# Where the exponents of a scan's weights lie, and which engine multiplies them by the weights

## The chip, the cores and the metric

The kernel runs on one core of a Trainium2 chip. A time is the device time of one execution in microseconds (us). The kernel before has a median of 2456.4 us over 3 runs (2455.82 to 2459.3).

## The reference, cut to what matters

One encoder layer runs on two requests with shared weights: a long one (prompt, 1024 tokens) and a short one (sample, 512 tokens). Half of its heads are a state space mixer with a scan in both directions, half are dilated attention; an output projection, a cross attention on 256 memory tokens and an MLP follow. All is in float32. The change lies in the scan, which goes over chunks of 128 tokens, one direction at a time, here forwards:

```python
a_cs = jnp.cumsum(dt * A.reshape(g, r), axis=2)
xdt = x * dt[..., None]
causal = jnp.tril(jnp.ones((q, q), dtype=bool))[:, :, None, None]
seg = a_cs[:, :, :, None] - a_cs[:, :, None, :]
lmat = jnp.where(causal, jnp.exp(jnp.where(causal, seg, 0.0)), 0.0)
cb = jnp.einsum('bcign,bcjgn->bcijg', Cm, Bm)
y_diag = jnp.einsum('bcijg,bcijgr,bcjgrp->bcigrp', cb, lmat, xdt)
...
y_off = jnp.einsum('bcign,bcgrpn,bcigr->bcigrp', Cm, prev, jnp.exp(a_cs))
return (y_diag + y_off).reshape(bsz, l, h, p)
```

There are 2 groups of 4 heads. The weights of a head inside a chunk, `cb * lmat * dt` summed over both directions, are a 128x128 matrix.

## The kernel before, in words

Dense work (projections, cross attention, MLP) runs on TensorE (PE) in three matmuls for each product, a high and a low part of every operand. Their weights arrive by DMA in pieces of 128x512 (`raw`), ScalarE (ACT) rounds them to the high part `whi` (L190), and VectorE (DVE) and GpSimd (POOL) take turns at the low part `wlo` (L192). The mixers are generators that are woven into this dense work: after so many dense steps comes one step of the mixer. The mixers run one after the other: scan of the short request, its attention, scan of the long one, its attention. The program text gives priorities only. A planner with its own timeline model (`schedule_with_timeline_sim=True`) orders the instructions of each engine before the program is built, and puts in the waits; on the chip each engine then works through its list in that order.

PSUM has eight banks of 128x512: three for dense sums (`mm`), two for transposes (`tp`), and one each for the tags `a`, `b`, `c` that the mixers share (`mx_bank`, tiles `ma`, `mb`, `mc`). A new tile of a tag waits until the last one of it has had its last reader.

In the scan, `ssd`, the short request has 4 chunks and the long one 8. The backward states come first. Then for every chunk c, in four steps:

1. `inside(c, 0)`: the first group's weights times the chunk's tokens, four heads, into bank `c` (`py`, L647). The rows of the next chunk's first group are asked for (`rows_of`, a DMA of 512 KB that spreads one row over 128 partitions, L628; its tile `se` has two buffers).
2. `inside(c, 1)` into the same bank; `masks` of the next chunk (bank `b`, L619 and L622); the rows of its second group; DVE adds the bank to `y` (L690); the carried state's part goes through bank `a` (`outside`, L656, L658).
3. `weigh(c + 1, 0)`: the weights of the next chunk's first group; the backward state's part through bank `b`.
4. `update` of the carried state (L594, L600, L601), `weigh(c + 1, 1)`, then the gate and the norm of the chunk (L702 to L708).

`weigh` has a tile `e` of 128x2x4x128: `e[:, 0]` holds the forward row sums, `e[:, 1]`, also called `w`, the backward ones, for each of four heads. For each head ACT makes the forward exponent in place (L635, Identity with a bias), DVE takes the smaller of it and the backward exponent (L636), ACT (L637) and DVE (L638) fill `w` with the masked products. Then one exponential over the four heads on ACT (L639) and one product `w * exp` on POOL (L640).

Of the kernel before, what the change touches and what calls it, by code (L numbers as in the profile page):

```python
# [13 lines left out]
AF = mybir.ActivationFunctionType  # L14
OP = mybir.AluOpType
# [69 lines left out]
def encoder(ctx: ExitStack, tc: tile.TileContext, I, y_p, y_s):  # L85
    nc = tc.nc
# [19 lines left out]
    def mx_bank(tag):  # L106
        return ps_mx.tile([128, 512], F32, name="m" + tag)
# [430 lines left out]
    def ssd(st, pool):  # L538
# [34 lines left out]
        def load(c, full):  # L573
            sl = slice(c * 128, c * 128 + 128)
            x = pool.tile([128, 512], F32, name="sx", bufs=2)
            nc.sync.dma_start(x, st.xs[sl, :])
            bt = pool.tile([128, 256], F32, name="sbt", bufs=2)
            nc.sync.dma_start(bt, st.bt[sl, :])
            if not full:
                return x, bt  # L580
            bc = pool.tile([128, 4, 128], F32, name="sbc", bufs=2)
            nc.sync.dma_start(bc, st.bc[:, sl].rearrange("(k p) t -> p k t", p=128))
            return x, bt, bc
# [21 lines left out]
        for c in range(nt - 1, 0, -1):  # L605
            x, bt = load(c, False)
# [23 lines left out]

        def weigh(c, g, cbm, e):
            w = e[:, 1]
            for h in range(4):
                col = [v[:, c, d * 8 + g * 4 + h:d * 8 + g * 4 + h + 1] for v in (nacs, st.dt) for d in range(2)]
                nc.scalar.activation(e[:, 0, h], e[:, 0, h], AF.Identity, bias=col[0])  # L635
                nc.vector.scalar_tensor_tensor(e[:, 0, h], w[:, h], col[1], e[:, 0, h], op0=OP.add, op1=OP.min)  # L636
                nc.scalar.activation(w[:, h], cbm[:, 1, g], AF.Identity, scale=col[3])  # L637
                nc.vector.scalar_tensor_tensor(w[:, h], cbm[:, 0, g], col[2], w[:, h], op0=OP.mult, op1=OP.add)  # L638
            nc.scalar.activation(e[:, 0], e[:, 0], AF.Exp)  # L639
            nc.gpsimd.tensor_tensor(w, w, e[:, 0], op=OP.mult)  # L640
            weights[c, g] = w

        def inside(c, g, py):
# [22 lines left out]
        for g in range(2):  # L666
            weigh(0, g, cbm, rows_of(0, g))
            yield
        for c in range(nt):
            nxt = c + 1 < nt  # L670
            sl = slice(c * 128, c * 128 + 128)
            x, bt, bc = tiles[c]
# [20 lines left out]
            if nxt:  # L693
                weigh(c + 1, 0, cbm, e0)
# [4 lines left out]
            if nxt:  # L699
                carry = update(carry, xs, bt, c, 0)  # L700
                weigh(c + 1, 1, cbm, e1)
# [584 lines left out]
```

## Time and profile before

| | |
|---|---|
| median of 3 runs | 2456.4 us |
| the profiled execution | 2455.78 us |
| its span, first to last instruction | 2454.0 us |
| PE busy | 2393.4 us (98%) |
| DVE busy | 1410.0 us (57%) |
| ACT busy | 967.3 us (39%) |
| POOL busy | 736.3 us (30%) |
| granted TensorE clock, mean | 0.993 |

A share over the whole span says little here, as the stages differ: the scans run in about 110 to 245 us (short request) and 545 to 735 us (long request), attention and dense work in the rest. A line of the profile names the line of the kernel (L640), the engine, and the tile written and read (`se<-se`). "Idle before" is the time in which the engine did nothing just before these instructions, with what ended it. DMAs are issued by the queue of SyncE (SP).

### The profile page before, as it was taken

The numbers are of one execution on the slowest core, as the hardware profiler recorded it, in microseconds if no ns is written. First come the engines' busy times: TensorE is split into PE (matmuls) and PEld (weight loads), VectorE is DVE, ScalarE is ACT, GpSimd is POOL, SyncE is SP. The second block draws the span as 40 slices with busy tenths as digits, with TensorE's granted clock in tenths as the row PEclk, the third lists the DMA queues.
The fourth block names the chain that finished last, engine by engine and source line by source line (L and its number), as shares of the span: only waits on it lengthen the run. The fifth ranks groups of instructions, "written<-read, shape, count | busy, mean of one in ns | idle before, by whom it ended". The sixth has DMA issues, their size and how long they took to land.

```text
span 2454.0 us, 34361 instructions
## 1 busy us (share of the span) xinstructions
PE 2393.4 (98%) x12323; PEld 2005.8 (82%) x12323; DVE 1410.0 (57%) x2834; ACT 967.3 (39%) x2337; POOL 736.3 (30%) x604
## 2 busy tenths in 40 slices
PE   7999999998889999999999999999999999999999
PEld 6877788887668997888878889999888888888887
DVE  7787677647885567556555635555534344344444
ACT  5465455445555556344423325334411212212111
POOL 3353214425542132333344212111222322222221
PEclk9999999999989999999999999999999999999999
DMA  5665345557766453344253411111111111211111
GB/s 184 192 213 191 118 136 148 147 170 245 239 234 177 111 142 93 105 122 112 74 191 104 172 35 53 56 56 44 35 52 35 52 52 39 65 35 52 52 35 69
DMA packets 253082, 272.00 MB, mean 111 GB/s; under 512 B 43090, under 2 KB 200048, under 8 KB 252912
## 3 DMA queue, kind: packets, MB, share of 16 engines
q1 hardware_dynamic: 252912, 269.82, 35.5%
q8 instruction: 97, 1.59, 0.3%
q14 instruction: 73, 0.60, 0.1%
HBM read 215.55 MB, written 54.20 MB: 110 GB/s over the span
## 4 chain that ended last, share of the span: by engine, by line
PE 78%; DMA 6%; DVE 5%; ACT 1%; issue 1%; SPq 1%; POOL 0%; ACTq 0%; DVEq 0%; POOLq 0%
PE mm L205 16%; PE mm L206 16%; PE mm L207 16%; PE tp L205 7%; PE tp L207 7%; PE tp L206 7%; PE mc L812 3%; PE ma L783 2%; DMA se<-acp 1%; PE mb L799 1%; DVE wlo L192 1%; PE tp L224 1%; DVE se L636 1%; DMA se<-acs 1%; DVE se L638 1%
## 5 line engine op out<-in xcount | busy, mean ns | idle before, releaser
L192 POOL TENSOR_TENSOR wlo<-raw,whi 128x512 fp32r<-128x512 f32 x240 | 361.5, 1521 | 520.7 <-ACT whi L190 447.9
L1138 DVE TENSOR_TENSOR h<-mm,h 128x512 f32<-128x512 f32 x384 | 262.6, 687 | 405.8 <-PE mm L207 405.3
L205 PE MATMUL mm<-whi,chi 128*128 128x512 f32 (+1 forms) x1088 | 397.1, 366 | 8.8 <-ACT chi L230 5.6
L206 PE MATMUL mm<-wlo,chi 128*128 128x512 f32 (+1 forms) x1088 | 392.2, 361 | 0.0
L207 PE MATMUL mm<-whi,clo 128*128 128x512 f32 (+1 forms) x1088 | 392.1, 363 | 0.0
L190 ACT CAST whi<-raw 128x512 fp32r<-128x512 f32 x480 | 268.2, 618 | 249.9 <-PE tp L206 115.8
L192 DVE TENSOR_TENSOR wlo<-raw,whi 128x512 fp32r<-128x512 f32 x240 | 294.3, 1238 | 102.6 <-ACT whi L190 102.2
L205 PE MATMUL mm<-whi,hidh 128*128 128x512 f32 x768 | 305.0, 397 | 0.8 <-DVE h L1138 0.8
L207 PE MATMUL mm<-whi,hidl 128*128 128x512 f32 x768 | 302.9, 394 | 0.0
L206 PE MATMUL mm<-wlo,hidh 128*128 128x512 f32 x768 | 302.5, 394 | 0.0
L205 PE MATMUL tp<-chi,whi 128*128 128x512 f32 x720 | 284.4, 395 | 0.0
L207 PE MATMUL tp<-chi,wlo 128*128 128x512 f32 x720 | 284.3, 395 | 0.0
L206 PE MATMUL tp<-clo,whi 128*128 128x512 f32 x720 | 284.0, 394 | 0.0
L1122 POOL TENSOR_TENSOR hidl<-hr,hidh 128x512 fp32r<-128x512 f32 x96 | 126.0, 1312 | 479.1 <-ACT hidh L1121 298.5
L205 PEld LDWEIGHTS mm<-whi,chi 128*128 128x128 f32 x1088 | 207.1, 190 | 39.2 <-ACT chi L230 7.0
L207 PEld LDWEIGHTS mm<-whi,clo 128*128 128x128 f32 x1088 | 206.5, 190 | 28.6
L206 PEld LDWEIGHTS mm<-wlo,chi 128*128 128x128 f32 x1088 | 206.9, 190 | 27.5
L1121 ACT CAST hidh<-hr 128x512 fp32r<-128x512 f32 x96 | 59.6, 621 | 400.1 <-PE mm L206 325.9
L205 PEld LDWEIGHTS mm<-whi,hidh 128*128 128x128 f32 x768 | 144.5, 188 | 34.1 <-DVE h L1138 1.8
L207 PEld LDWEIGHTS mm<-whi,hidl 128*128 128x128 f32 x768 | 144.4, 188 | 33.6
L206 PEld LDWEIGHTS mm<-wlo,hidh 128*128 128x128 f32 x768 | 144.6, 188 | 32.3
L207 PEld LDWEIGHTS tp<-chi,wlo 128*128 128x128 f32 x720 | 135.4, 188 | 31.5
(285 smaller groups left out, 4109.0 us busy)
## 6 DMA issues: line engine op xcount, KB each, us to landing
raw<-in_mlp_w_dram SPq DMA_DIRECT2D x256, 256.0 KB
raw<-in_w_in_dram SPq DMA_DIRECT2D x96, 256.0 KB
qkp<-ev SPq DMA_DIRECT2D x32, 256.0 KB
raw<-in_xatt_wkv_dram SPq DMA_DIRECT2D x32, 256.0 KB
se<-acp SPq DMA_DIRECT2D x16, 512.0 KB
raw<-in_w_out_dram SPq DMA_DIRECT2D x32, 256.0 KB
ak<-qkp SPq DMA_DIRECT2D x32, 256.0 KB
raw<-in_xatt_wq_dram SPq DMA_DIRECT2D x32, 256.0 KB
```

Source lines behind the costliest of these rows:

```text
L190: nc.scalar.copy(hi[:, sl, sc], raw)
L192: eng.tensor_tensor(lo[:, sl, sc], raw, f(hi[:, sl, sc]), op=OP.subtract)
L205: nc.tensor.matmul(ps, lh, rh, start=start, stop=False)
L206: nc.tensor.matmul(ps, lh, rl, start=False, stop=False)
L207: nc.tensor.matmul(ps, ll, rh, start=False, stop=stop)
L224: nc.tensor.transpose(pt[:, k, t, :], xn[t][:, (2 * kp + k) * 128:(2 * kp + k + 1) * 128], units(2 * kp + k))
L636: nc.vector.scalar_tensor_tensor(e[:, 0, h], w[:, h], col[1], e[:, 0, h], op0=OP.add, op1=OP.min)
L783: nc.tensor.matmul(pq[:, i, :W], qu, ops[i][0][j], start=j == 0, stop=j == 1)
L812: nc.tensor.matmul(po[:, i * 64:i * 64 + 64], pT[:, i * nk + j, :], ops[i][1][j][:, rs], start=j == 0, stop=j == nk - 1)
L1121: nc.scalar.copy(hh[:, ft], r)
L1122: nc.gpsimd.tensor_tensor(hl[:, ft], r, f(hh[:, ft]), op=OP.subtract)
L1138: nc.vector.tensor_tensor(h[t][:, cs], ps, h[t][:, cs], op=OP.add)
```

## The change

The exponents are written to a PSUM tile `x` of tag `c`, the tag of the chunk's sum `py`, instead of back into `e[:, 0]`. ACT writes them there, DVE takes the minimum there, ACT's exponential runs there in place. The product with the weights moves from POOL to DVE, with one input in SBUF and one in PSUM. Everything behind these lines has numbers that are two higher.

```diff
         def weigh(c, g, cbm, e):
             w = e[:, 1]
+
+            x = mx_bank("c").rearrange("p (h i) -> p h i", h=4)
             for h in range(4):
                 col = [v[:, c, d * 8 + g * 4 + h:d * 8 + g * 4 + h + 1] for v in (nacs, st.dt) for d in range(2)]
-                nc.scalar.activation(e[:, 0, h], e[:, 0, h], AF.Identity, bias=col[0])
-                nc.vector.scalar_tensor_tensor(e[:, 0, h], w[:, h], col[1], e[:, 0, h], op0=OP.add, op1=OP.min)
+                nc.scalar.activation(x[:, h], e[:, 0, h], AF.Identity, bias=col[0])
+                nc.vector.scalar_tensor_tensor(x[:, h], w[:, h], col[1], x[:, h], op0=OP.add, op1=OP.min)
                 nc.scalar.activation(w[:, h], cbm[:, 1, g], AF.Identity, scale=col[3])
                 nc.vector.scalar_tensor_tensor(w[:, h], cbm[:, 0, g], col[2], w[:, h], op0=OP.mult, op1=OP.add)
-            nc.scalar.activation(e[:, 0], e[:, 0], AF.Exp)
-            nc.gpsimd.tensor_tensor(w, w, e[:, 0], op=OP.mult)
+            nc.scalar.activation(x, x, AF.Exp)
+            nc.vector.tensor_tensor(w, w, x, op=OP.mult)
             weights[c, g] = w
```

## Rows read from the trace of the kernel before

**Rows 1.** The page, busy time and share of the span by engine.
```profile
PE 2393.4 (98%) x12323; PEld 2005.8 (82%) x12323; DVE 1410.0 (57%) x2834; ACT 967.3 (39%) x2337; POOL 736.3 (30%) x604
```

**Rows 2.** Windows: busy us by engine, granted clock, DMA share, of both scans.
```profile
core 0: us, PE busy (x) PEld busy (x) DVE busy (x) ACT busy (x) POOL busy (x), PEclk, DMA share, GB/s
110.00:245.00 135.00, 127.53 (x622) 104.33 (x621) 105.66 (x224) 80.01 (x185) 67.19 (x67) 0.99 0.63 200
...
545.00:735.00 190.00, 165.74 (x776) 132.37 (x775) 157.27 (x307) 103.92 (x293) 100.49 (x83) 0.94 0.73 241
```

**Rows 3.** Waits of PE in 545:735: us in total, times, longest us.
```profile
PE ma L656 <- DVE carry L601: 5.2, 3, 3.8
PE mc L647 <- POOL se L640: 4.7, 4, 2.3
```

**Rows 4.** Timeline of PE: start, us, instructions, idle time before and what ended it.
```profile
662.19 1.10 PE L647 MATMUL mc<-sx,se 128*128 128x64 f32 x8 [2.29 <-POOL se L640]
...
680.03 1.12 PE L647 MATMUL mc<-sx,se 128*128 128x64 f32 x8 [1.60 <-POOL se L640]
```

**Rows 5.** Windows of 5 us behind these two waits, columns as in rows 2.
```profile
660.00:665.00 5.00, 2.81 (x14) 2.48 (x15) 4.58 (x8) 3.43 (x8) 4.36 (x3) 0.89 0.37 110
665.00:670.00 5.00, 5.00 (x19) 3.97 (x19) 3.14 (x8) 0.95 (x2) 2.32 (x3) 0.77 0.88 215
...
680.00:685.00 5.00, 4.97 (x21) 4.33 (x22) 5.00 (x7) 3.12 (x9) 2.53 (x2) 0.66 0.16 40
```

**Rows 6.** Lines of POOL, 110:245 and 545:735: busy us, mean ns, idle before.
```profile
L640 POOL TENSOR_TENSOR se<-se 128x512 f32<-128x512 f32 x8 | 11.6, 1444 | 11.4 <-DVE se L638 5.0 <-DVE rst L212 4.0 <-ACT ev L522 2.3
...
L640 POOL TENSOR_TENSOR se<-se 128x512 f32<-128x512 f32 x16 | 21.0, 1315 | 25.1 <-DVE se L638 7.3 <-ACT chi L230 6.4 <-ACT ev L906 3.0
```

**Rows 7.** Lines of DVE in 545:735, columns as in rows 6.
```profile
L636 DVE SCALAR_TENSOR_TENSOR se<-se,sa 128x128 f32<-128x128 f32 x64 | 29.1, 504 | 14.3 <-ACT se L635 14.1
L638 DVE SCALAR_TENSOR_TENSOR se<-scbm,dtp,se 128x128 f32<-128x128 f32 x64 | 27.9, 478 | 0.0
L192 DVE TENSOR_TENSOR wlo<-raw,whi 128x512 fp32r<-128x512 f32 x18 | 21.0, 1179 | 3.7 <-ACT whi L190 3.7
...
L690 DVE TENSOR_TENSOR sy<-mc,sy 128x512 f32<-128x512 f32 x8 | 5.4, 681 | 0.6 <-PE mc L647 0.6
```

**Rows 8.** Three lines of DVE, whole span: ns minimum/median/maximum, first and last start.
```profile
L636 DVE SCALAR_TENSOR_TENSOR se<-se,sa x96: 335/343/1430, 117.4 to 723.0; 128x128 f32<-128x128 f32 x96
L638 DVE SCALAR_TENSOR_TENSOR se<-scbm,dtp,se x64: 333/340/1387, 562.2 to 729.2; 128x128 f32<-128x128 f32 x64
...
L587 DVE TENSOR_TENSOR sxs<-sx,sdd x20: 673/680/1542, 92.1 to 699.3; 128x512 f32<-128x512 f32 x20
```

**Rows 9.** Timelines of DVE and ACT; then the line of ACT's L230 in 545:735.
```profile
638.80 0.47 DVE L907 SCALAR_TENSOR_TENSOR ev<-tp,gqk,ev 128x256 fp32r<-128x256 f32 x1
...
639.31 0.47 ACT L906 ACTIVATE ev<-tp,gqk 128x256 fp32r<-128x256 f32 x1 [4.70 <-DVE ev L907]
...
L230 ACT ACTIVATE chi<-tp,cols 128x256 fp32r<-128x256 f32 x24 | 10.9, 470 | 18.3 <-DVE clo L231 9.7 <-PE tp L224 8.6
```

**Rows 10.** Timelines by engine, one turn of the long request's scan, in order of time.
```profile
605.41 0.40 SPq L628 DMA_DIRECT2D se<-acp  x1
605.52 1.00 PE L647 MATMUL mc<-sx,se 128*128 128x64 f32 x8
...
609.62 0.68 DVE L690 TENSOR_TENSOR sy<-mc,sy 128x512 f32<-128x512 f32 x1
610.00 1.28 ACT L635 ACTIVATE se<-se,sa 128x128 f32<-128x128 f32 x4 [2.85 <-DMA se<-acp]
610.43 3.01 DVE L636 SCALAR_TENSOR_TENSOR se<-se,sa 128x128 f32<-128x128 f32 x4
...
617.66 1.27 POOL L640 TENSOR_TENSOR se<-se 128x512 f32<-128x512 f32 x1 [0.81 <-POOL wlo L192]
618.99 1.10 PE L647 MATMUL mc<-sx,se 128*128 128x64 f32 x8 [0.54 <-POOL se L640]
...
626.94 1.00 PE L647 MATMUL mc<-sx,se 128*128 128x64 f32 x8
```

## The prediction

> **What bounds the kernel now.** I read the page first, then the windows, then who TensorE (PE) waits for, then the lines of the scan. The page shows PE busy for 2393.4 of 2454.0 us and VectorE (DVE) for 1410.0 [rows 1]: what the program can give back, beside PE work that this change does not touch, is 60.6 us of PE idle time and some time at the lower clock. The windows say where it lies: the scan of the short request runs in 110:245 and that of the long one in 545:735. PE is idle for 135.00 - 127.53 = 7.5 us in the first and for 190.00 - 165.74 = 24.3 us in the second, where the granted clock is 0.94, so about 0.06 x 190 = 11 us more go there [rows 2]. DVE is busy for 83% of the second window, POOL for 53%. So the scan windows are held up by late inputs, not by an engine at its peak, and the whole prize is some 43 us, 1.7% of the time.
>
> Of the waits of PE in 545:735 two matter: 5.2 us for the carry (DVE), and 4.7 us, in four waits, for the product of the weights on POOL, L640 [rows 3]. [...]
>
> **The change, part by part.** One call of weigh makes the weights of four heads; there are 8 calls for the short request and 16 for the long one, 24 in all.
>
> *POOL's product goes.* It took 21.0 + 11.6 = 32.6 us, 1.3 to 1.4 us a piece [rows 6]. The waits of PE on it, 4.7 + 3.4 = 8.1 us with the clock, end if the new product is there earlier by 2.29 us. It should be: a DVE operation on 128x512 with one input in PSUM takes 0.68 us (L690), 0.6 less than POOL's, and L636 in front of it gets shorter, next. From 8.1 saved to 0 (the waits come back under another name); I take the 8.1.
>
> *L636 gets its second input and its output in PSUM.* Today both inputs lie in SBUF; its median is 343 ns but its longest 1430, and in 545:735 the mean is 504 [rows 7, 8]. DVE operations with one PSUM input hardly spread there: L690 has a mean of 681 ns. So the long ones are those that meet POOL at SBUF, and L636 leaves that group: 29.1 - 64 x 0.343 = 7.1 us less. L638 keeps both inputs in SBUF, with 27.9 - 64 x 0.340 = 6.1 us of excess, as L192 does with 21.0 - 18 x 0.68 = 8.8; L640 is 21.0 of POOL's 100.5 us in that window [rows 2], so about a fifth of these 14.9 us, 3.1 us, goes too. Against it DVE gets 16 x 0.681 = 10.9 us for the products. Net in 545:735: +0.7 us on 157. DVE is neither relieved nor loaded there; I take 0, between -5 (all of the excess of L638 and L192 that L640 may cause in its own neighbourhood) and +10.9. In 110:245 the eight products cost 5.4 us of DVE, and PE has no wait on L640 there to win back. DVE has 29 us of slack in that window; I take 0.5 us, between 0 and 5.4.
>
> On the price of a PSUM operand the row shows no difference: L690, from the bank, has a mean of 681 ns, and L587, with both inputs in SBUF and the same 128x512, a median of 680 [rows 7, 8]. [...]
>
> *L635 and the exponential (L639) write to PSUM.* No row has either with its output there. ACT is busy for 104 of 190 us, so that some 0.1 us more or less on each of 80 instructions hides in its slack: 0, between -5 and +5.
>
> *ACT and DVE now take turns in one bank.* Today the four L635 run back to back (1.28 us from 610.00) while L636 follows [rows 10]. In the keys of the cross attention ACT and DVE read two halves of one bank, with no data passing from DVE to ACT, and there the trace has L906 of the second half waiting 4.70 us for L907 of the first [rows 9]. So I expect L635 of head 2 to wait for L636 of head 1, and so on: three more handovers in each call, 72 in all. The same handover in the transposes, L230 behind L231, left ACT idle for 9.7 us in 24 instructions, 0.40 us a piece [rows 9]; 72 x 0.40 = 29 us on the path of the weights. What is queued behind a waiting L635 is ACT's other work: PSUM evacuations and casts of weights, for which PE waits in the end. Today L640 itself waits for 25.1 + 11.4 = 36.5 us [rows 6], and 4.7 us of that reach PE, 13%. The same share of 29 is 3.8 us. From 0 to 29; I take 3.8.
>
> *The bank is the accumulator's.* Until now the two groups of a chunk overlap, and the matmuls of the first group (L647) need only their own weights. Now the second call cannot start before the first one's product has read the bank, the first call not before L690 has read the chunk's sum, and neither group's matmuls before both calls are through. One turn of the loop, read from 605.52 to 626.94: 21.4 us [rows 10]. The rows of the first group are asked for at 605.41 and there at 610.00; its call lasts from 610.00 to 618.93, 8.9 us. L690 ends at 610.3, so it holds nothing back. Inside the call the four L636 took 3.01 us, against 4 x 0.343 = 1.4; without that and with 0.6 off the product a call takes 6.7 us. Two in a row: 610.0 + 13.4 = 623.4, and the 16 matmuls end 2.1 us later, at 625.5, before the 627.9 of today. So by this turn the loop costs 0. At its present 8.9 us a call it would end at 629.9, 2.0 us late; there are 3 + 7 = 10 such turns, so 20 us is the other end. I take 0, as L636 must leave the group with the spread.
>
> *POOL's queue.* 32.6 us of work and 36.5 us of waiting in front of it leave POOL. L600 (the carry) and half of the L192 stand in that queue; PE waits 5.2 us for the carry. I take a quarter, 1.3 us, between 0 and 5.2.
>
> **The sum.** -8.1 + 0.5 + 3.8 + 0 - 1.3 = -5.1 us. The profiled execution took 2455.8 us (span 2454.0, 1.8 around it), 0.6 under the median of the runs. I expect 2455.8 - 5.1, about 2450.5 us.
>
> **Rivals.**
> 1. *The bank makes the loop longer: slower.* Place: L647 of the first group, which PE meets in order, with dense matmuls queued behind it. It decides at 7.9 us a call: (627.9 - 610.0 - 2.1) / 2. Above that every turn ends late. At 8.9 us: 10 x 2.0 = 20 us of PE waits, and behind waits of such length 1.7 us each at the lower clock (0.55 + 1.15 after the one at 662.19), 17 us; less the 8.1 saved. That is +12 to +29, middle about 2474 us. For it: the handovers, 1.2 us a call if each costs its 0.40, which would bring 6.7 to exactly 7.9. Against it: the order of the instructions is planned again with the new waits, and the planner can put dense matmuls before L647. [...]
> 2. *No change: PE waits anyway.* The waits on L640 come when DVE is late, and DVE is as busy as before; what PE no longer waits for here it waits for at the next DVE result (carry, syo). 2456 us. For it: DVE's net load of +0.7 us. Against it: the lower clock behind the two long waits is an own loss.
> 3. *Much faster.* DVE's results come when they were planned, and half of the second window's 24.3 + 11.4 us comes back: 2438 us. For it: the spread of every DVE operation with two SBUF inputs. Against it: four fifths of POOL's work there stay.
>
> **How the numbers follow.** Forecast 47%, rival 1 28%, rival 2 18%, rival 3 7%. A measurement of this kernel tells 0.2%, 4.9 us, from no change. The forecast lies at that edge with its own range of 2442 to 2455: of its 47 I count 35 as faster and 12 as the same. Rival 1: 24 slower, 4 the same. Rival 2: 2 faster, 13 the same, 3 slower. Rival 3: faster. Together 0.44, 0.29, 0.27. For 8 in 10 the range takes in rival 3 at 2438 and most of rival 1, up to 2472.
>
> **What would show it.** In the changed profile: no product of the weights on POOL, POOL's busy time down by about 33 us; 24 DVE products of about 0.68 us; L636 (two lines lower) with a longest of less than 0.5 us instead of 1.43; L635 no longer in runs of four, but each behind an L636 in the waits of ACT; a call of under 7.9 us; PE idle time in the long request's scan below 24 us, without the waits of 1.6 and 2.3 us at L647. I am wrong if L636 still spreads up to 1.4 us with its input in PSUM, if a call takes longer than 7.9 us, or if PE's waits at L647 grow in number: then rival 1 holds.

## The result, and the profile after

The changed kernel has a median of 2433.1 us (2430.5 to 2433.5, 4 runs) against 2457.6 us for the kernel before in the same comparison; the ratio is 0.990, with a 95% interval of 0.988 to 0.991. It is 25 us faster, where 5 were forecast, and the time lies outside the range of the prediction. The profiled execution took 2430.5 us, with a span of 2428.7 us.

The page's line of busy time, of the changed kernel, answers to [rows 1]:

```profile
PE 2382.5 (98%) x12323; PEld 2001.8 (82%) x12323; DVE 1401.8 (58%) x2858; ACT 973.7 (40%) x2337; POOL 705.0 (29%) x580
```

The span is shorter by 25.3 us. PE's idle time went from 2454.0 - 2393.4 = 60.6 to 46.2 us, so 14.4 us are waits that are gone. The other 10.9 us are PE's busy time: the same 12323 matmuls, and less of it at the lower clock (granted mean 0.996 instead of 0.993, some 7 us of it). POOL lost 31.3 us and 24 instructions.

The windows of both scans in the changed kernel, with the columns of [rows 2]:

```profile
110.00:245.00 135.00, 130.59 (x643) 107.13 (x642) 100.03 (x209) 76.99 (x171) 56.91 (x58) 1.00 0.63 202
545.00:735.00 190.00, 181.16 (x872) 148.43 (x871) 152.99 (x304) 107.15 (x284) 85.38 (x72) 0.98 0.75 252
```

In the second window PE is idle for 8.8 us instead of 24.3, at a granted clock of 0.98 instead of 0.94. The scan of the changed kernel goes on to 774 us, that of the kernel before to 732, so this window leaves out its end; in 545 to 780 PE is idle for 13.8 us instead of 25.2. Here is who PE waits for in 545 to 735, the changed kernel's answer to [rows 3] (us in total, times, longest us):

```profile
PE mb L619 <- DMA sbc<-bcp: 3.7, 2, 2.6
PE mm L205 <- ACT chi L230: 3.1, 2, 2.2
PE ma L594 <- DVE syo L660: 0.9, 2, 0.7
PE mc L649 <- DVE se L642: 0.6, 1, 0.6
```

The reader should add such a list up by the engine that ended the wait. Before, of 24.1 us 12.5 were waits on DVE, 4.7 on POOL, 3.9 on ACT, 1.6 on DMAs and 1.4 on nothing that shows. The waits on DVE before, beside the carry of [rows 3]:

```profile
PE ma L594 <- DVE syo L658: 2.0, 3, 0.9
PE tp L903 <- DVE ev L901: 2.0, 3, 0.8
PE mb L619 <- DVE sy L702: 1.9, 1, 1.9
...
PE tp L224 <- DVE clo L231: 1.4, 1, 1.4
```

After, of 8.8 us 2.0 are on DVE, none on POOL, 3.1 on ACT and 3.7 on DMAs. The waits on POOL's product, on which the forecast rests, are a third of what went; two thirds are waits on DVE. The total is firm, but such a split is not. Run n below has the instructions of the kernel before in the same order, and in the same window it has 23.3 us of waits, of which 7.9 are on DVE, 5.6 on POOL and 4.5 on DMAs:

```profile
PE mc L647 <- POOL se L640: 5.6, 3, 2.3
PE ma L656 <- DVE carry L601: 3.0, 3, 1.7
```

The changed kernel's lines of DVE in 545 to 735, with the columns of [rows 7]:

```profile
L192 DVE TENSOR_TENSOR wlo<-raw,whi 128x512 fp32r<-128x512 f32 x24 | 29.7, 1253 | 6.3 <-ACT whi L190 6.3
L640 DVE SCALAR_TENSOR_TENSOR se<-scbm,dtp,se 128x128 f32<-128x128 f32 x52 | 24.7, 475 | 7.1 <-ACT se L639 6.5
L638 DVE SCALAR_TENSOR_TENSOR mc<-se,sa,mc 128x128 f32<-128x128 f32 x52 | 18.1, 348 | 14.6 <-ACT mc L637 14.6
L642 DVE TENSOR_TENSOR se<-se,mc 128x512 f32<-128x512 f32 x12 | 8.2, 682 | 0.6
```

And four operations over the whole span (ns minimum/median/maximum, first and last start), two of DVE and two of ACT in the changed kernel, to be read against [rows 8]:

```profile
L638 DVE SCALAR_TENSOR_TENSOR mc<-se,sa,mc x96: 340/348/358, 116.7 to 768.6; 128x128 f32<-128x128 f32 x96
...
L642 DVE TENSOR_TENSOR se<-se,mc x24: 672/680/689, 151.0 to 769.9; 128x512 f32<-128x512 f32 x24
...
L637 ACT ACTIVATE mc<-se,sa x96: 350/354/383, 115.4 to 767.9; 128x128 f32<-128x128 f32 x96
...
L641 ACT ACTIVATE mc<-mc x24: 576/578/591, 123.4 to 769.3; 128x512 f32<-128x512 f32 x24
```

then the same two of ACT in the kernel before:

```profile
L635 ACT ACTIVATE se<-se,sa x96: 384/388/405, 116.0 to 722.1; 128x128 f32<-128x128 f32 x96
...
L639 ACT ACTIVATE se<-se x24: 613/618/631, 119.7 to 727.1; 128x512 f32<-128x512 f32 x24
```

The reader compares the first and the last of the three times: the min (L638) never takes more than 358 ns; before, it went up to 1430. The reader should also see what did not become narrow: L640, with both inputs in SBUF, has a mean of 475 ns (478 before), and L192 one of 1253 (1179 before).

The starts and ends in the traces also show what the long operations meet. Before, 16 of the 96 min operations take more than 400 ns, and every one of them overlaps work of POOL, on average for 93% of its time; of the other 80, 62 overlap none. In the changed kernel 19 of the 96 run entirely beside work of POOL, and none is long.

The last view is one turn of the long request's scan, the answer to [rows 10]: ACT and DVE alternate in the bank, and the second call begins when the first one's product has ended.

```profile
607.23 2.00 PE L649 MATMUL mc<-sx,se 128*128 128x64 f32 x16 [0.63 <-DVE se L642]
...
614.19 0.68 DVE L692 TENSOR_TENSOR sy<-mc,sy 128x512 f32<-128x512 f32 x1
...
616.08 0.37 ACT L637 ACTIVATE mc<-se,sa 128x128 f32<-128x128 f32 x1 [1.29 <-DMA se<-acp]
618.16 0.34 DVE L638 SCALAR_TENSOR_TENSOR mc<-se,sa,mc 128x128 f32<-128x128 f32 x1
...
624.26 0.67 DVE L642 TENSOR_TENSOR se<-se,mc 128x512 f32<-128x512 f32 x1
625.00 0.35 ACT L637 ACTIVATE mc<-se,sa 128x128 f32<-128x128 f32 x1
...
634.00 0.68 DVE L642 TENSOR_TENSOR se<-se,mc 128x512 f32<-128x512 f32 x1
635.41 1.78 PE L649 MATMUL mc<-sx,se 128*128 128x64 f32 x15
```

A turn is longer than before: the seven turns from the first to the last L649 take 27.4 us each (580.6 to 772.5), where those of L647 took 21.2 (582.4 to 731.0). In PE's instruction list 93 dense matmuls stand in a turn, on average, where there were 46. The scan takes longer, and PE waits less for it.

### The profile page after: what moved, and what is told of

Same layout as the page of the kernel before. It is cut to its first block, busy times and chain, and to the rows that moved or that the text cites. A ratio compares the mean times of both kernels' runs of the same rounds, so it can differ in the third digit from the quotient of the medians.

```text
span 2428.7 us, 34338 instructions
## 1 busy us (share of the span) xinstructions
PE 2382.5 (98%) x12323; PEld 2001.8 (82%) x12323; DVE 1401.8 (58%) x2858; ACT 973.7 (40%) x2337; POOL 705.0 (29%) x580
## 3 DMA queue, kind: packets, MB, share of 16 engines
q1 hardware_dynamic: 252912, 269.82, 35.7%
## 4 chain that ended last, share of the span: by engine, by line
PE 67%; DVE 4%; DMA 3%; ACT 1%; issue 1%; SPq 0%; POOL 0%; DVEq 0%; ACTq 0%; POOLq 0%
PE mm L205 13%; PE mm L206 13%; PE mm L207 13%; PE tp L205 7%; PE tp L206 7%; PE tp L207 7%; PE mc L814 2%; PE ma L785 1%; PE mb L801 1%; DVE wlo L192 1%; PE tp L224 1%; DMA nclp<-ano 0%; DMA se<-acp 0%; PE tp L1009 0%; DMA acl<-nclp 0%
## 5 line engine op out<-in xcount | busy, mean ns | idle before, releaser
L192 POOL TENSOR_TENSOR wlo<-raw,whi 128x512 fp32r<-128x512 f32 x240 | 361.8, 1524 | 549.0 <-ACT whi L190 490.7
L192 DVE TENSOR_TENSOR wlo<-raw,whi 128x512 fp32r<-128x512 f32 x240 | 292.5, 1229 | 103.9 <-ACT whi L190 103.5
L206 PEld LDWEIGHTS mm<-wlo,hidh 128*128 128x128 f32 x768 | 144.6, 188 | 32.7
L205 PEld LDWEIGHTS mm<-whi,hidh 128*128 128x128 f32 x768 | 144.4, 188 | 32.7
L206 PEld LDWEIGHTS tp<-clo,whi 128*128 128x128 f32 x720 | 135.5, 188 | 31.1
```

Source lines behind the costliest of these rows:

```text
L192: eng.tensor_tensor(lo[:, sl, sc], raw, f(hi[:, sl, sc]), op=OP.subtract)
L205: nc.tensor.matmul(ps, lh, rh, start=start, stop=False)
L206: nc.tensor.matmul(ps, lh, rl, start=False, stop=False)
```

## The experiments

Five theories were to be told apart. **1, ports:** the min had two SBUF inputs and met POOL there; with one in PSUM it is narrow, and DVE's results come in time. **2, room:** the bank's lock makes each turn longer, so that the planner sets more dense matmuls ahead of L649, and a late result meets no idle PE. **3:** it is the product's move to DVE alone. **4:** it is the turn-taking of ACT and DVE alone. **5:** the narrow min and the room are both needed.

The table gathers all runs. A turn is the mean of the long scan's seven, "dense" the dense matmuls in PE's list for one turn, "min" the mean of L636 or what stands for it in 545 to 900. "Waits on DVE" are PE's in 545 to 900. "Lost" is PE's idle time plus (1 - granted clock) of each window of 5 us (10 us behind 900): in 110 to 290 (the short scan) and in 545 to 900, and in the last column in 545 to 780 (the long scan, which in s and u runs on past that) and in 780 to 1240 (mostly the attention behind it). The times of the ratios are medians, and all other columns come from one profiled execution.

| kernel | ratio to before, interval | turn, us | dense | min, ns | waits on DVE, us | lost, us | lost in 545 to 780; 780 to 1240, us |
|---|---|---|---|---|---|---|---|
| before | 1 | 21.2 | 46 | 504 | 14.7 | 9.3; 39.1 | 37.1; 11.1 |
| changed | 0.990 (0.988 to 0.991) | 27.4 | 93 | 348 | 5.5 | 5.8; 19.3 | 17.2; 11.9 |
| p_rate_after | 0.991 (0.989 to 0.993) | 27.4 | 93 | 347 | 5.7 | 8.3; 18.5 | 15.9; 11.8 |
| s_bank_a | 0.991 (0.989 to 0.993) | 32.9 | 117 | 348 | 5.8 | 6.1; 28.6 | 15.2; 18.4 |
| g_pool_dummy | 0.994 (0.992 to 0.995) | 28.3 | 93 | 348 | 9.6 | 6.4; 22.9 | 20.4; 15.8 |
| f_min_into_bank | 0.995 (0.993 to 0.997) | 26.0 | 71 | 486 | 14.7 | 2.7; 35.7 | 32.7; 11.8 |
| r_turns_min_bank | 0.996 (0.995 to 0.998) | 27.6 | 89 | 443 | 9.0 | 5.5; 29.9 | 20.5; 25.5 |
| w_four_by_four | 0.996 (0.995 to 0.998) | 27.4 | 89 | 350 | 8.0 | 8.8; 28.7 | 19.4; 25.5 |
| c_exp_only_bank | 0.998 (0.997 to 1.000) | 22.8 | 63 | 355 | 7.2 | 15.3; 30.4 | 30.4; 11.7 |
| n_replan | 1.000 (0.999 to 1.002) | 21.3 | 46 | 512 | 9.9 | 11.7; 39.8 | 36.5; 12.6 |
| a_prod_dve | 1.001 (0.999 to 1.002) | 20.3 | 46 | 431 | 9.4 | 14.9; 33.2 | 31.7; 13.0 |
| g2_pool_dummy_before | 1.001 (1.000 to 1.002) | 21.8 | 47 | 574 | 17.0 | 12.7; 48.9 | 43.9; 15.5 |
| h_turns_sbuf | 1.002 (1.001 to 1.003) | 23.9 | 64 | 460 | 16.4 | 9.5; 40.0 | 36.1; 19.2 |
| m_rate_before | 1.002 (1.001 to 1.003) | 22.5 | 51 | 474 | 9.2 | 10.6; 44.0 | 39.8; 14.6 |
| v_pace_before | 1.002 (1.001 to 1.004) | 26.2 | 75 | 439 | 11.4 | 10.2; 26.7 | 25.7; 16.7 |
| b_exps_bank_pool | 1.003 (1.002 to 1.004) | 26.3 | 82 | 347 | 6.5 | 18.0; 22.6 | 19.4; 26.0 |
| j_two_banks | 1.004 (1.003 to 1.006) | 23.1 | 53 | 347 | 19.0 | 12.7; 54.9 | 52.0; 10.7 |
| k_tp_bank | 1.006 (1.004 to 1.008) | 23.2 | 56 | 347 | 15.2 | 8.5; 48.0 | 46.5; 15.9 |
| q_rate_tp_bank | 1.008 (1.006 to 1.010) | 24.7 | 65 | 347 | 15.5 | 14.3; 56.2 | 50.2; 20.3 |
| u_all_in_bank | 1.008 (1.006 to 1.011) | 39.6 | 134 | 350 | 12.6 | 8.3; 40.3 | 21.9; 28.6 |

Three pairs of traces run the same order of instructions, and so show by how much two executions of one order differ: before and n throughout, on every engine and in the queue of DMAs; changed and p up to 874 us; k and q, on PE and DVE, up to 616 us. The waits on DVE differ by up to 4.8 us, the loss of the short scan by up to 5.8 (k, q), that of the long one by no more than 1.3.

**The product alone** (a; against the kernel before):

```diff
-            nc.gpsimd.tensor_tensor(w, w, e[:, 0], op=OP.mult)
+            nc.vector.tensor_tensor(w, w, e[:, 0], op=OP.mult)
```

> The kernel before with the product of the weights on VectorE instead of GpSimd, everything still in SBUF. Theory 1 (ports): the gain of 1.0% comes from VectorE no longer meeting GpSimd at SBUF; here L636 keeps both inputs in SBUF and only GpSimd's product goes, so about -5 us (2452). Theory 2 (slack): the gain comes from the bank's lock, by which the planner puts the two groups of a chunk in a row and sends dense matmuls ahead of L647; no lock here, so 0 +- 5 us (2457). Theory 3 (GpSimd's product alone): -20 to -25 us (2435).

No change, 1.001. Its product from SBUF, over the whole span, is not narrow as L642 is:

```profile
L640 DVE TENSOR_TENSOR se<-se x24: 676/680/1676, 152.1 to 729.8; 128x512 f32<-128x512 f32 x24
```

The long scan loses 6 us less, near the forecast's first term. The short one loses 6 us more, where 0.5 was set; two executions of one order can differ by nearly that. Theory 3 falls.

**The exponents in the bank, the product left on POOL** (b; against before):

```diff
+            x = mx_bank("c").rearrange("p (h i) -> p h i", h=4)
...
+                nc.scalar.activation(x[:, h], e[:, 0, h], AF.Identity, bias=col[0])
+                nc.vector.scalar_tensor_tensor(x[:, h], w[:, h], col[1], x[:, h], op0=OP.add, op1=OP.min)
...
+            nc.scalar.activation(e[:, 0], x, AF.Exp)
```

> Identity and minimum in the bank, the exponential goes from the bank back to SBUF, the product stays on GpSimd. Theory 1 (ports): L636 leaves the contention, L640 stays: -10 to -15 us (2445). Theory 2 (slack): the bank is held from the first Identity to the exponential, turns of the long scan over 25 us as in the changed kernel: -20 us (2437). Theory 3 (product): 0 +- 5 us (2457).

Slower, 1.003, and yet the long scan loses 22.6 us in 545 to 900, nearly as little as in the changed kernel. The loss lies in the short scan (18.0 us, twice that of before) and in the attention behind 900 us (22.9 us against 9.0 before). So the bank's part makes the gain in the long scan, without the product's move. That the move is needed in the short scan is not shown: a, which has it, loses 14.9 us there.

**Only the exponential in the bank** (c), and **the min written into the bank from two SBUF inputs** (f), both with the product on DVE; against the changed kernel:

```diff
 c
-                nc.scalar.activation(x[:, h], e[:, 0, h], AF.Identity, bias=col[0])
-                nc.vector.scalar_tensor_tensor(x[:, h], w[:, h], col[1], x[:, h], op0=OP.add, op1=OP.min)
+                nc.scalar.activation(e[:, 0, h], e[:, 0, h], AF.Identity, bias=col[0])
+                nc.vector.scalar_tensor_tensor(e[:, 0, h], w[:, h], col[1], e[:, 0, h], op0=OP.add, op1=OP.min)
...
-            nc.scalar.activation(x, x, AF.Exp)
+            nc.scalar.activation(x, e[:, 0], AF.Exp)
 f
-                nc.scalar.activation(x[:, h], e[:, 0, h], AF.Identity, bias=col[0])
-                nc.vector.scalar_tensor_tensor(x[:, h], w[:, h], col[1], x[:, h], op0=OP.add, op1=OP.min)
+                nc.scalar.activation(e[:, 0, h], e[:, 0, h], AF.Identity, bias=col[0])
+                nc.vector.scalar_tensor_tensor(x[:, h], w[:, h], col[1], e[:, 0, h], op0=OP.add, op1=OP.min)
```

> Identity and minimum stay in SBUF, only the exponential's output lies in the bank, VectorE multiplies from there. Theory 1 (ports): L636 stays spread (longest over 1.3 us), GpSimd's product goes: -5 us (2452). Theory 2 (slack): the bank is held from the exponential to the product only, groups overlap as before, a turn of about 22 to 24 us: -5 to -10 us (2449). Theory 3 (product): -20 to -25 us (2435).

> As the changed kernel, but ScalarE's Identity stays in SBUF, so that the minimum reads two SBUF inputs and only its output and the exponential lie in the bank; ScalarE and VectorE take no turns head by head. Theory 1 (ports): L636 spreads again up to 1.4 us, so at most -5 to -8 us (2450). Theory 2 (slack): the lock is that of the changed kernel, a turn of 25 us and more: -20 to -25 us (2435). Theory 3 (product): -20 to -25 us.

The times are 0.998 and 0.995. The min of f spreads as before, though it writes to PSUM:

```profile
L638 DVE SCALAR_TENSOR_TENSOR mc<-se,sa x96: 344/358/1405, 116.0 to 754.0; 128x128 f32<-128x128 f32 x96
```

So it is the input in PSUM that makes it narrow (358 ns at most in the changed kernel), not the output (1405 here). With the lock and turns of 26.0 us, but a wide min, the long scan still loses 35.7 us in 545 to 900: against theory 2 in its pure form. But its turns hold 71 dense matmuls and not 93; r, below, has 89 and a wide min. In c the min is narrow nearly throughout, since POOL has little to do beside it (91 of the 96 overlap no work of POOL), and with 63 dense matmuls in a turn the loss is 30.4 us.

**The turn-taking alone, in SBUF** (h; against before), and **the kernel before planned anew** by putting the request for the second group's rows ahead of `masks` (n):

```diff
 h
-                nc.scalar.activation(e[:, 0, h], e[:, 0, h], AF.Identity, bias=col[0])
-                nc.vector.scalar_tensor_tensor(e[:, 0, h], w[:, h], col[1], e[:, 0, h], op0=OP.add, op1=OP.min)
+                t = pool.tile([128, 128], F32, name="srow", bufs=1)
+                nc.scalar.activation(t, e[:, 0, h], AF.Identity, bias=col[0])
+                nc.vector.scalar_tensor_tensor(e[:, 0, h], w[:, h], col[1], t, op0=OP.add, op1=OP.min)
 n
-                cbm = masks(c + 1)
                 e1 = rows_of(c + 1, 1)
+                cbm = masks(c + 1)
```

> The kernel before, but ScalarE's Identity of each head goes to one small SBUF tile that all heads share, so that ScalarE and VectorE take turns head by head as they do in the bank; minimum, exponential and GpSimd's product stay in SBUF. Theory 1 (ports: L636 no longer meets GpSimd at SBUF): no relief here, L636 spreads up to 1.4 us, 2457 +- 5 us, and 30 us or more lost in 545:780. Theory 4 (pace: the turns by themselves spread the scan's work and let PE run on): as much as the changed kernel has there, 16 to 18 us lost in 545:780, -15 us (2442).

> The kernel before with the request for the second group's rows moved ahead of the masks in the program text: no work changes, but the planner orders everything anew. All theories: 2457 us; what it differs is the size of a plan's own luck, up to 5 us.

The times are 1.002 and 1.000. Turn-taking by itself gains nothing, and theory 4 falls as a cause by itself. Run n missed its aim: its trace has every instruction of PE, DVE, ACT and POOL, and every DMA of SyncE's queue, in the order of the kernel before. It is that kernel run again, and says nothing of what another order is worth.

**A second POOL product in each call**, with an output that nothing reads; in the changed kernel (g) and in the kernel before (g2):

```diff
+            nc.gpsimd.tensor_tensor(e[:, 0], e[:, 0], e[:, 0], op=OP.mult)
```

> The changed kernel with one more GpSimd product in each call, of the old size, whose result nobody reads (it squares the row sums in place after the last Identity). Theory 1 (ports): GpSimd's load is that of before, L640 and L192 spread more again, L636 stays narrow: 5 to 8 us of the 25 go (2440). Theory 2 (slack by the bank's lock): nothing goes, 2433 +- 3 us.

> The kernel before with a second POOL product in each call, behind the first, on SBUF alone (24 operations of 1.3 us more). Theory 1 (ports): the added operations meet DVE's two-input operations, DVE busy grows by some 5 to 10 us, the loss in the scan windows grows by 5 to 20 us: 2462 to 2478 us. Theory 2: POOL has room, and no order on PE changes by it: 2456 to 2461 us.

24 POOL operations give back 8 us, by the medians, of the changed kernel's gain (0.994), while PE's list has the same 93 dense matmuls in a turn; the loss in 545 to 780 goes from 17.2 to 20.4 us. In the kernel before they cost 3 us (1.001), less than theory 1 said, although DVE's 64 + 64 operations grow by 4.4 + 3.9 us against [rows 7], here in g2, 545 to 780 (its profiled execution, of 2469 us, is its slowest; the median is 2461.6):

```profile
L636 DVE SCALAR_TENSOR_TENSOR se<-se,sa 128x128 f32<-128x128 f32 x64 | 33.5, 574 | 17.0 <-ACT se L635 17.0
L638 DVE SCALAR_TENSOR_TENSOR se<-scbm,dtp,se 128x128 f32<-128x128 f32 x64 | 31.8, 536 | 0.0
```

That POOL work in SBUF stretches DVE's operations with two SBUF inputs is shown: in n, with the order of the kernel before, the min's mean is 512 ns against 504, here it is 574. A microsecond of DVE is not a microsecond of the kernel, though.

**Another bank for the exponents:** a transpose bank (k), heads in turn in bank `c` and a transpose bank (j), bank `a` (s); against the changed kernel:

```diff
 k
-            x = mx_bank("c").rearrange("p (h i) -> p h i", h=4)
+            x = tp_bank().rearrange("p (h i) -> p h i", h=4)
 s
-            x = mx_bank("c").rearrange("p (h i) -> p h i", h=4)
+            x = mx_bank("a").rearrange("p (h i) -> p h i", h=4)
 j
+            xs = [mx_bank("c").rearrange("p (h i) -> p h i", h=4), tp_bank().rearrange("p (h i) -> p h i", h=4)]
...
+                x, i = xs[h % 2], h // 2
```

> The changed kernel with the exponents in a bank of the transposes (two buffers) instead of the accumulator's, so that the two groups may overlap and the chunk's sum holds nothing up. Theory 1 (ports): the gain stays or grows, turns of 21 to 25 us, 2425 to 2435 us. Theory 2 (slack by the lock): most of the gain goes, 2450 us; the dense transposes may also wait for the bank.

> The changed kernel with the heads in two banks in turn, the accumulator's and one of the transposes, so that ScalarE writes one while VectorE works in the other; two exponentials and two products of half the size. The lock by the accumulator stays and L636 stays narrow. Theory 5: as the changed kernel, 2433 to 2440 us (24 more instructions on each of two engines, two banks of the transposes held). If the turns of ScalarE and VectorE in one bank made the gain: 2450 us.

> As the changed kernel, but the exponents lie in bank a, which the carried state's part uses, instead of the accumulator's bank c. Theory 1 (ports): the min is narrow and the product is on DVE, so the time is that of the changed kernel, 2431 to 2438 us. Theory 2 (it is the lock with the chunk's sum that lets dense matmuls go ahead of L649): the lock is with another, shorter tenant, turns below 25 us, 2445 to 2456 us. Theory 5: between, by how long the turns become.

Bank `a` does as well as the accumulator's (0.991), against what theory 2 expected of a shorter tenant: its turns are even longer, 32.9 us, with 117 dense matmuls. So theory 2's guess at the turn was wrong, and its mechanism was not. A transpose bank makes it slower (1.006 and 1.004) with the same narrow min, and turns of 23 us. Who PE waits for in k, 545 to 900:

```profile
PE mb L619 <- DMA sbc<-bcp: 7.7, 3, 3.9
PE mm L205 <- ACT mm L944: 3.2, 1, 3.2
PE ma L594 <- DVE tp L638: 2.9, 1, 2.9
```

The dense work's transposes share that tag, so that these two runs change a second thing. They show that a narrow min alone is not enough, not why.

**The memory's part woven with 0.6 instead of 0.8 steps of the mixer for each dense step:** before (m), changed (p), with the transpose bank (q).

```diff
-        weave(mixing, 0.8, memory(pool, lambda: mixed(S, range(2), atA)), 0.5)
+        weave(mixing, 0.6, memory(pool, lambda: mixed(S, range(2), atA)), 0.5)
```

> The kernel before with one number changed: the scan gets 0.6 instead of 0.8 steps for each step of the dense work beside the long scan, so that its turns should grow from 21 to about 26 us without any bank or port in play. Theory 2 (slack: longer turns are enough): 16 to 22 us lost in 545:780 instead of 37, 2440 us. Theory 5 (both are needed, longer turns and a narrow L636): about as much lost there as in the run that only puts the minimum into the bank, 32 us, 2452 us. Theory 1 (ports alone): 2457 us.

> The changed kernel with the scan at 0.6 steps beside the long scan. Theories 2 and 5: the lock sets a turn of 27 us already, so 0 +- 4 us (2433). If still longer turns help: 2425.

> The exponents in a bank of the transposes, so no lock between the groups, and the scan at 0.6 steps. Theory 5: narrow L636 and longer turns together, about 20 us lost in 545:780 instead of 47, 2440 us. If the bank of the transposes itself was what cost 13 us, the loss stays over 35 us, 2465 us.

This missed its aim: turns grew by 1.3 us (m), 0.0 (p) and 1.5 (q), so that room was hardly varied. Nor is p another order of the scans: it runs as the changed kernel does up to 874 us, and it shows that the gain comes again (0.991).

**The min's input put back to SBUF under the same lock and turn-taking** (r; against the changed kernel):

```diff
-                nc.scalar.activation(x[:, h], e[:, 0, h], AF.Identity, bias=col[0])
-                nc.vector.scalar_tensor_tensor(x[:, h], w[:, h], col[1], x[:, h], op0=OP.add, op1=OP.min)
+                t = pool.tile([128, 128], F32, name="srow", bufs=1)
+                nc.scalar.activation(t, e[:, 0, h], AF.Identity, bias=col[0])
+                nc.vector.scalar_tensor_tensor(x[:, h], w[:, h], col[1], t, op0=OP.add, op1=OP.min)
```

> As the changed kernel, with one difference: L637 writes the forward exponent to a tile of SBUF with one buffer, and the min of L638 reads its two inputs from SBUF and writes to bank c. The turn-taking of ACT and DVE, the bank's lock, the exponential in the bank and the product on DVE stay. Theory 1 (ports: the min must have an input in PSUM to be narrow): L638 spreads again up to 1.4 us; some 30 us of lost PE time (idle plus clock) in 545 to 780 instead of 16; 2445 to 2450 us. Theory 5 (both the narrow min and the long turns are needed) expects the same. Theory 2 (only the lock and the turns of 27 us count): L638 may spread, but the loss stays near 16 us and the time at 2432 to 2437 us.

The time is 0.996: 16 of the 25 us are lost again, nearly as theories 1 and 5 said (2450.9 us, where they said 2445 to 2450). The two DVE operations of a head in r, 545 to 780:

```profile
L639 DVE SCALAR_TENSOR_TENSOR mc<-se,sa,srow 128x128 f32<-128x128 f32 x64 | 28.4, 443 | 17.7 <-ACT srow L638 17.4
...
L641 DVE SCALAR_TENSOR_TENSOR se<-scbm,dtp,se 128x128 f32<-128x128 f32 x64 | 27.2, 425 | 7.1 <-ACT se L640 6.7
```

But they had the loss in the wrong place: in 545 to 780 they expected some 30 us, and it is 20.5, close to the 17.2 of the changed kernel and the 15.9 of p, as theory 2 said. The rest appears just behind it, up to 900 us (9.4 us against 2.1), and in the attention after that (16.1 us in 900 to 1240 against 9.8).

**Four L637, then four L638** (w; against changed), one handover in place of four:

```diff
+            for h in range(4):
+                nc.scalar.activation(x[:, h], e[:, 0, h], AF.Identity, bias=cols4[h][0])
             for h in range(4):
...
-                nc.scalar.activation(x[:, h], e[:, 0, h], AF.Identity, bias=col[0])
```

> As the changed kernel, but the four L637 of a call are issued ahead of its four L638, so that ACT and DVE hand the bank over once a call instead of four times; lock, narrow min and product on DVE stay. The planned order of PE still has some 85 dense matmuls in a turn of the long scan, as the changed kernel has (the kernel before: 55, the run with the min written into the bank from two SBUF inputs: 71). Theory 5 (a narrow min and many dense matmuls in a turn are both needed, the handovers by themselves are not): lost PE time in 545 to 900 of 15 to 22 us, as 19 in the changed kernel, 2426 to 2437 us. Theory 4 (the handovers between ACT and DVE are what paces the scan): more loss, as in the run with the min written into the bank (36 us in 545 to 900), 2440 to 2450 us.

The time is 0.996 (2449.1 us), in the range of theory 4, and the loss of 28.7 us in 545 to 900 lies between what the two theories expected. The turn stays at 27.4 us, so it does not hang on the number of handovers. In the scan little is lost, 19.4 us in 545 to 780. The operations behind the min now run back to back with no idle time before them, and are longer (a mean of 525 ns; in the changed kernel, over the same 64, it is 451); w in 545 to 780:

```profile
L642 DVE SCALAR_TENSOR_TENSOR se<-scbm,dtp,se 128x128 f32<-128x128 f32 x64 | 32.6, 525 | 0.8 <-ACT se L641 0.8
...
L640 DVE SCALAR_TENSOR_TENSOR mc<-se,sa,mc 128x128 f32<-128x128 f32 x64 | 22.4, 350 | 2.3 <-ACT mc L637 1.8
```

The rest is lost behind the scan, as in r: 25.5 us in 780 to 1240 in both, against 11.9. From 778 to some 950 us r and w run one and the same order on PE, and not that of the changed kernel, with PE waiting at the same places; the longest wait in 780 to 900, first of r, then of w:

```profile
PE ma L786 <- DMA aq<-qkp: 3.3, 1, 3.3
```

```profile
PE ma L787 <- DMA aq<-qkp: 2.5, 1, 2.5
```

The min is wide in r and narrow in w. So most of the 16 us that each of them loses cannot be put down to the min, nor to the handovers: it comes with the order of what follows the scan.

**Room alone** (v; against before), the long scan woven more thinly:

```diff
             nc.sync.dma_start(st.mix[sl, 0:512], y)
             yield
+            if st is R:
+                yield
...
-        weave(mixing, 0.8, memory(pool, lambda: mixed(S, range(2), atA)), 0.5)
+        weave(mixing, 0.35, memory(pool, lambda: mixed(S, range(2), atA)), 0.5)
```

> The kernel before with the long request's scan woven more thinly into the dense work, and nothing else: one more empty step in each of its turns, and 0.35 instead of 0.8 steps for each dense step beside the memory's keys and values. The planned order of PE has 56, 38, 52, 138, 96, 84, 84 and 48 dense matmuls between the chunks instead of some 55 throughout. No bank, no lock; the product stays on POOL, the min stays in SBUF and spreads. Theory 2 (the number of dense matmuls in a turn alone decides): the thin turns lose little, the loss in 545 to 900 falls from 39 to 20 to 28 us, and the time to 2437 to 2448 us. Theories 1 and 5 (the min must be narrow as well): the waits on L640 and L636's followers stay, 33 to 42 us there, 2452 to 2464 us. The attention that follows is displaced by this, which can cost up to 10 us behind 780.

The loss in 545 to 900 falls from 39.1 to 26.7 us, as theory 2 said, though the min is wide (439 ns) and there is no bank: room is a cause by itself. But the time is 1.002, in the range of theories 1 and 5. The attention ends so late that a later projection waits for its output; PE's waits of v in 1240 to 2400:

```profile
PE tp L224 <- DMA xn<-mixp: 9.8, 4, 5.9
```

**Both DVE operations narrow** (u; against changed), two heads at a time, ACT's scaled product in the bank's other half:

```diff
+            x = mx_bank("c").rearrange("p (k h i) -> p k h i", k=2, h=2)
+            for h0 in (0, 2):
+                for i in range(2):
...
+                    nc.scalar.activation(x[:, 1, i], cbm[:, 1, g], AF.Identity, scale=col[3])
...
+                    nc.vector.scalar_tensor_tensor(w[:, h], cbm[:, 0, g], col[2], x[:, 1, i], op0=OP.mult, op1=OP.add)
+                nc.scalar.activation(x[:, 0], x[:, 0], AF.Exp)
+                nc.vector.tensor_tensor(w[:, h0:h0 + 2], w[:, h0:h0 + 2], x[:, 0], op=OP.mult)
```

> A further version: two heads at a time, the forward exponents in one half of bank c and ACT's scaled product in the other half, so that both DVE operations of a head (L638 and L640) have one input in PSUM; two exponentials and two products of half the size in each call. Theory 1 (ports): L640 becomes narrow as well (mean 0.34 instead of 0.40 to 0.48 us), some 5 to 6 us of DVE time go in the long scan, against 24 more products at a fixed cost of some 0.1 to 0.2 us; 2425 to 2435 us. Theory 2: longer turns do no harm by themselves; turn of 28 to 32 us, 2430 to 2445 us, where above 28 us a turn the room ends as in the run with an added POOL operation (2441).

Slower, 1.008. Both operations are narrow (351 and 345 ns in 545 to 780). A product of half the size takes 412 ns in 540 to 900, two of them 824 where the changed kernel's one takes 682, so that each of the 24 more products costs 0.14 us, within the 0.1 to 0.2 expected. But a turn takes 39.6 us, DVE waits for ACT, and PE waits 9.5 us for the attention's output at the end, as in v:

```profile
L641 DVE SCALAR_TENSOR_TENSOR mc<-se,sa,mc 128x128 f32<-128x128 f32 x44 | 15.4, 351 | 25.4 <-ACT mc L640 25.2
L642 DVE SCALAR_TENSOR_TENSOR se<-scbm,dtp,mc 128x128 f32<-128x128 f32 x44 | 15.2, 345 | 1.0
```

No run beat the changed kernel; p and s equal it.

## Why the prediction was wrong

The direction was right, the size was off by a factor of five, and where most of the gain comes from was not among the terms of the sum. (The sum as written gives 2450.7 us, which changes nothing.) By its own steps:

- **POOL's product.** As forecast: the waits on it are gone, POOL has 31.3 us less, the 24 products on DVE take 680 ns each. As a term of the sum, 8.1 us, it is right for what it names: the move alone (a) loses 5 to 6 us less in the long scan, and more in the short one. The 3.4 us in it are an estimate from [rows 5], (0.11 + 0.23 + 0.34) x 5, what the clock of the three slices lacks of 1; in the kernel before it reads 0.50 in 664 to 667 and in 681 to 684. No run shows this term by itself; what the changed kernel shows is 0.98 instead of 0.94 over the whole second window.
- **L636.** The narrowing came as forecast, and at no price for the PSUM operand: medians of 348 ns against 343 for the min, and of 680 against 680 for the product. The prediction's "DVE is neither relieved nor loaded there; I take 0" balanced busy times, whereas PE asks when a result is there. But the runs give the narrowing no large value either: r, with a wide min under the same lock and 89 dense matmuls, loses 20.5 us in 545 to 780, w with a narrow one 19.4, changed and p 17.2 and 15.9. That is 1 to 5 us in the long scan.
- **The relief of L638 and L192** (3.1 us) did not come: means of 475 and 1253 ns against 478 and 1179. It did no harm to the sum, as the balance was set at 0 anyway.
- **ACT's writes to PSUM**, set at 0 between -5 and +5: L637 takes 354 ns instead of 388, the exponential 578 instead of 618, some 4 us less on ACT in all (96 x 0.034 + 24 x 0.040). Where the input lies in SBUF, the bank was the faster destination, for L637 and for the exponential of c (586 ns). With the input in the bank the exponential takes 578 ns into the bank and 579 into SBUF (b), which is no difference.
- **Handovers.** They are there, though not where the prediction looked: L637 stands behind L639 in ACT's list, and so the wait appears at L639. Waits of ACT in 545 to 735, the changed kernel first and then the one before:

```profile
ACT se L639 <- DVE mc L638: 26.0, 34, 1.8
```

```profile
ACT se L637 <- DVE se L636: 13.4, 11, 3.8
```

  The first line holds 52 heads, since the changed scan goes on behind 735 us; up to 780, over all 64, it is 26.3 us, and the second stays 13.4. So 0.41 us for each head, against 0.21. With three handovers to four heads that is an estimate of 0.27 us a handover, where 0.40 was taken. In w, with one handover a call, it is 10.9 us. PE paid nothing that shows for them.
- **The accumulator's bank. This is the step that failed:** "So by this turn the loop costs 0", between 0 and 20 us of loss. It put the lock into today's order of instructions, where it can only delay. The call takes 8.9 and 9.7 us (616.08 to 624.93, 625.00 to 634.68), above the 7.9 from which rival 1 was to decide; the 6.7 of the forecast left out the 1.2 us of handovers that its sum charges elsewhere. By the prediction's own sign rival 1 should then have held, and its mechanism did come true: the loop is 6.2 us a turn longer. Its price did not: PE waits 0.6 us in all at L649 in 545 to 735, since the planner put 93 dense matmuls in a turn instead of 46. The argument against rival 1 in the prediction names this, but gave it no gain.

  It has the largest one: the loss in 545 to 780 goes from 37.1 to 17.2 us, where all of the kernel's loss, summed in the same way, goes from 73.3 to 50.3. This loss falls as the dense matmuls in a turn grow. With 82 to 93 it is 16 to 20.5 us, with the narrow min (changed, p, g, w, b), with the wide one (r) and with the product on POOL (b). With 71 to 75 and a wide min it is 25.7 (v, with no exponents in a bank) and 32.7 (f). With 46 to 56 it is 32 to 52 us, with a wide min as with a narrow one (j, k). The runs between, with 63 to 65, have 30.4 (c), 36.1 (h) and 50.2 (q, in a transpose bank).
- **Rival 3**, with 7% and 2438 us, came nearest to the outcome: of the second window's loss two thirds come back (24.3 + 11.4 us before, 8.8 + 3.8 after), where it said half. What spoke against it, that four fifths of POOL's work stay in SBUF, was no bar. Its reason, results of DVE that come as planned, is not what the runs bear out first.

So for the long scan theory 2 stands nearest: the room that the lock makes gives most of what is gained there, and the narrow min a little. For the kernel's time that is not enough. b, r and w lose about as little in the long scan (19.4 to 20.5 us), but 25.5 to 26.0 us behind it, where the changed kernel loses 11.9, little more than the kernel before with 11.1. v pays 16.7 us there, and 19 us more in 1240 to 2400, where the kernel before loses 2. That so little is lost behind the scan in the changed kernel is not explained by anything in the change; p loses as little there, although its order is another one from 979 us on. As far as the runs show, this part is luck. So of the 23 us of loss that went, 20 went in the long scan, and nothing to speak of was lost behind it; the 3.5 us of the short scan are within what two executions of one order can differ. What stays open is why the attention comes in a worse order in b, r and w. That a transpose bank undoes the gain is measured (1.006 in k), its cause is not.

## What to carry to other kernels

Where late results and not a busy engine hold PE up, count the independent matmuls that stand in one turn of the loop; the one wait that names the edited line is only a part. A tenant that locked a bank lengthened the loop (from 21.2 us a turn to 27.4 in bank `c` and 32.9 in bank `a`), but as the order was planned anew with independent matmuls at hand, the longer loop lost less (19.3 and 28.6 us in 545 to 900 instead of 39.1). Its limit is the next stage, which must not come too late, as in v and u (waits of 9.8 and 9.5 us for the attention's output). Where a planner orders everything anew, compare losses by stage before putting a difference in time down to the edit: r and w lost most of their 16 us in a stage that the edit does not touch. And check that a run meant as another order is one: n was not.

## What the runs showed of the hardware

- The min, a VectorE operation of 128x128, hardly spreads with one input in PSUM (340 to 358 ns over 96; means of 347 and 348 in the other banks), also beside POOL's work (19 of the 96 run entirely beside it); with both inputs in SBUF it does (335 to 1430 in the kernel before), even when its output is in PSUM (344 to 1405 in f), and it grows with POOL's work (504 to 574 ns in the mean with 24 POOL operations more). The longest in the kernel before takes some four times the median (1430 to 343 ns).
- The long ones are among those that meet POOL: all 16 min operations of the kernel before that take over 400 ns overlap its work, but so do 18 of the 80 others, so meeting it is not enough. In c 5 of 96 overlap it, two of these are long (the longest 1356 ns), and the mean in the long scan is 355 ns.
- Both ScalarE operations of the change take 32 to 40 ns less with PSUM on at least one side: the Identity 354 ns from SBUF into the bank against 388 in SBUF; the exponential 618 in SBUF, 586 from SBUF into the bank (c), 579 from the bank into SBUF (b), 578 in the bank.
